# Feed-forward out-projections as seven block products, with weight block sums made by adding DMAs

## The chip, the cores and the metric

The kernel runs on one core of a Trainium2 chip, in one launch. The metric is the device time of one execution in microseconds. Before the change the median of three runs is 1543.88 us (1541.49 to 1548.66). The engines are TensorE (PE, with its weight loads shown as PEld), VectorE (DVE), ScalarE (ACT), GpSimd (POOL) and SyncE (SP). DMAs are put on a queue by SP, ACT or POOL, and sixteen DMA engines carry them.

## The reference, cut to what matters

The model is a two-layer streaming encoder over 640 frames: 512 of a prompt and 8 x 16 of running streams. Layer 0 is a convolution module, layer 1 is banded attention; each is followed by a SwiGLU feed-forward block. Everything is float32.

```python
D_MODEL, SEQ, DEPTH, DEC_BATCH, DEC_SEQ = 1024, 512, 2, 8, 16
FFN_HIDDEN = 2816                       # 22 tiles of 128

def swiglu_ffn(h, g, w_in, w_out):      # once in each layer
    a, b = jnp.split(rms_norm(h, g) @ w_in, 2, axis=-1)
    return h + (jax.nn.silu(a) * b) @ w_out
```

So each feed-forward block multiplies 640 x 1024 by 1024 x 5632 (the in-projection), gates, and multiplies 640 x 2816 by 2816 x 1024 (the out-projection).

## The kernel before, in words

The residual `h` stays in SBUF, features on the partitions: 8 tiles of 128 features by 640 frames. The frames are handled as two halves of 320 columns.

Float32 accuracy comes from splitting. ACT rounds a tensor to a `hi` part in the matmul's fast float32 type, DVE subtracts it from the original and so makes the `lo` part (`hilo`, L319, and `xsplit`, L153). Every product is then three matmuls: hi by hi, lo by hi, hi by lo.

`ffn` (L284) runs once per layer. An inner tile is 128 of the 2816 hidden features, with its `a` and its `b` column of the in-projection; its weights are four blocks of 128 x 512 floats, one megabyte in all. The first three inner tiles (NSTD) are done plainly (`std`, L391: 96 matmuls each). The other 19 go through `seven` (L401). It treats the in-projection of one tile as a 2 x 2 by 2 x 2 block product, rows being `a` and `b`, columns being the two halves of the frames, and forms it from seven block products instead of eight: 7 x 4 x 3 = 84 matmuls of 128 x 320. That needs sums of weight blocks, made in `w_seven` (L339): one load of the raw megabyte, then four additions or subtractions of 512 columns on DVE (L352), then the split into hi and lo of all seven operands. The sums of the activations, XT1 to XT4, are made once per layer. The last two products of a tile are issued by `after`, inside the next tile's `seven`.

The out-projection is plain. The 22 inner tiles are done in groups of 6, 6, 6 and 4 (`F1`, L40, loop at L493). After a group's gated tiles are in place, its out-weights are loaded in five pieces, split, and `mm3` (L162) accumulates over the group for each of 8 output tiles and 2 halves; DVE adds each result from PSUM to `h` (L530). The last group's columns are cut by `tail` instead of by half.

Each engine runs its own instructions in order. The order is made at build time by a list scheduler with a model of times; `tc.high_priority` moves splits, gates and evictions forward. Raw weights have two buffers (`wp`, bufs=2), and so have the split ones; the six PSUM buffers `mm` hold the accumulators. SP issues the weight loads in order and waits before each until the last reader of the buffer, on DVE, is done.

Of the kernel before, what the change touches and what calls it, by code (L numbers as in the profile page):

```python
# [8 lines left out]
F32 = mybir.dt.float32  # L9
# [6 lines left out]
P = 128  # L16
# [23 lines left out]
F1 = ((0, 6), (6, 6), (12, 6), (18, 4))  # L40
# [17 lines left out]
CW = 6  # L58
# [15 lines left out]
def tile_trunk(ctx, tc, xT, vecs, hist, w_pw1, w_pw2, w_in0, w_out0, w_in1, w_out1,  # L74
# [11 lines left out]
    tw = [320]  # L86
    mm = tps.enter_context(tc.tile_pool(name="mm0", bufs=4, space=PSUM))
# [81 lines left out]
    def square(s, n, eng="a", q=None):  # L169
        if q is None:  # L170
            q = tp.tile([P, tw[0]], F32, tag="sq", name=nm("sq"))
# [10 lines left out]
    def colmean(st, pieces, n, cut, tag, eng=nc.gpsimd, accp=None):  # L182
# [3 lines left out]
        for s in pieces[:cut]:  # L186
# [3 lines left out]
            if acc is None:  # L190
                acc = accp or tp.tile([P, tw[0]], F32, tag="acc", name=nm("acc"), bufs=1)
# [92 lines left out]
    def ffn(l, w_in, w_out, tail, hf):  # L284
# [15 lines left out]
        bcw = xo.tile([P, NT], F32, name=nm("bcw"), tag="bcw")  # L300
# [6 lines left out]
        xb = ExitStack()  # L307
        xt = xb.enter_context(tc.tile_pool(name="xt", bufs=1, reuse_waits="tile"))

        def hidt(jj, dt=F32R):  # L310
            return [hpf.tile([P, 2, NH], dt, tag=f"h{t}{jj}", name=nm("hid")) for t in "hl"]
# [4 lines left out]
        def wsmall(n=1024, t="v"):  # L316
            return [wx.tile([P, n], F32R, tag=t + x, name=nm(t + x)) for x in ("hi", "lo")]

        def hilo(hi, lo, a, src):  # L319
            b = a + src.shape[-1]  # L320
            nc.scalar.activation(out=hi[:, a:b], in_=src, func=AF.Copy)  # L321
            nc.vector.tensor_tensor(out=lo[:, a:b], in0=src, in1=hi[:, a:b].bitcast(F32),  # L322
                                    op=ALU.subtract)

        def w_std(src, small):
            raw = wp.tile([P, 2048], F32, tag="raw", name=nm("raw"))
            ws = []
            for i in range(2):
                if small or i == 0:
                    hi, lo = (wsmall if small else wbig)()  # L330
                o = 0 if small else 1024 * i
                nc.sync.dma_start(raw[:, 1024 * i:1024 * i + 1024], src[:, 1024 * i:1024 * i + 1024])
                with tc.high_priority(offset=HP):
                    hilo(hi, lo, o, raw[:, 1024 * i:1024 * i + 1024])
                ws.append((hi, lo, o))
            return {X11: ws[0][:2] + (ws[0][2],), X21: ws[0][:2] + (ws[0][2] + 512,),
                    "b": (ws[1], ws[1][:2] + (ws[1][2] + 512,))}

        def w_seven(src):  # L339
            raw = wp.tile([P, 2048], F32, tag="raw", name=nm("raw"))  # L340
            nc.sync.dma_start(raw, src)
            a11, a12, a21, a22 = (raw[:, 512 * i:512 * i + 512] for i in range(4))
            s1 = wx.tile([P, 512], F32, tag="s1", name=nm("s1"), bufs=1)
            vh, vl = wsmall()
            uh, ul = wsmall(512, "u")
            gh, gl = wbig()
            sub, add = ALU.subtract, ALU.add
            with tc.high_priority(offset=HP):
                hilo(vh, vl, 0, raw[:, 0:1024])
                for out, x, y, op in ((s1, a21, a22, add), (a21, a11, a21, sub),  # L350
                                      (a11, s1, a11, sub), (a12, a12, a11, sub)):
                    nc.vector.tensor_tensor(out=out, in0=x, in1=y, op=op)  # L352
# [3 lines left out]
            return {X11: (vh, vl, 0), X21: (vh, vl, 512), X22: (gh, gl, 512), XT2: (gh, gl, 0),  # L356
                    XT1: (gh, gl, 1536), XT3: (gh, gl, 1024), XT4: (uh, ul, 0)}

        def product(pt, w, x, first):
            wh, wl, o = w  # L360
            for k in range(4):
                a, b = wh[:, o + k * P:o + k * P + P], wl[:, o + k * P:o + k * P + P]
                for i, (wt, v) in enumerate(((a, XH), (b, XH), (a, XL))):
                    nc.tensor.matmul(pt, wt, v[x][:, k, :], start=(first and k == i == 0),  # L364
                                     stop=(k == 3 and i == 2), skip_group_check=True)
# [10 lines left out]
        def plus(tag, kept, pt):  # L376
            t = ftmp(tag)
            with tc.high_priority(offset=HP):
                nc.vector.tensor_tensor(out=t, in0=pt, in1=kept, op=ALU.add)
# [6 lines left out]
        def gate(t, a, b, hid):  # L386
            with tc.high_priority(offset=HP):
                nc.vector.tensor_tensor(out=t, in0=a, in1=b, op=ALU.mult)
                xsplit(t, *hid)

        def std(ws, half, hid):  # L391
            pa, pb = mmt()[:, :NH], mmt()[:, :NH]
            for x, ka, kb in (((X11, X11, 0), (X21, X21, 1)), ((XT4, X11, 0), (X22, X21, 1)))[half]:
                product(pa, ws[ka], x, kb == 0)
                product(pb, ws["b"][kb], x, kb == 0)
# [820 lines left out]
```

## Time and profile before

| | |
|---|---|
| median of 3 runs | 1543.88 us |
| span of the profiled execution | 1541.4 us |
| PE busy in the span | 1480.1 us, 96% |
| DVE, ACT, POOL busy | 994.1, 668.7, 229.8 us |
| moved by DMA | 163.14 MB, mean 106 GB/s |
| PE clock granted, mean | 0.986 |

The profile's lines give engine, operation, tiles out<-in, shape, count, busy time and mean duration in ns, then how long the engine sat idle just before them and what ended that. A matmul's own duration is longer than the distance from one to the next, since they are pipelined: counts in a stretch of time tell the rate. Feed-forward of layer 0 lies at about 270 to 690 us of the span, that of layer 1 at about 1095 to 1530 us.

### The profile page before, as it was taken

Reading aid. Unit: us, or ns where it says so; the run is one execution under the profiler, and the core shown is the slowest. Engines: PE = TensorE matmul, PEld = TensorE weight load, DVE = VectorE, ACT = ScalarE, POOL = GpSimd, SP = SyncE. Lnnn points to the kernel's source line nnn. Section 1 sums busy time; section 2 is a strip of 40 time slices with the busy share of each in tenths; the row PEclk is TensorE's granted clock in tenths of the full one; section 3 lists DMA queues with packets and bytes.
Section 4 is the critical chain, followed back from the end, with each engine's and each line's share of the span. In section 5 each row is a group of like instructions: output and inputs, shape, how many; then the busy total and the mean of one; then the engine's idle time right before and its main releaser. Section 6 shows DMA issues by size and latency. Waiting matters only on the chain.

```text
span 1541.4 us, 27271 instructions
## 1 busy us (share of the span) xinstructions
PE 1480.1 (96%) x11190; PEld 1409.6 (91%) x11190; DVE 994.1 (64%) x1963; ACT 668.7 (43%) x1293; POOL 229.8 (15%) x250
## 2 busy tenths in 40 slices
PE   5999899999999999999999999988999999999997
PEld 5998689999999999999987798857899999999996
DVE  5799346775575575566776668553776575575556
ACT  3666245443353353344664355442544253253233
POOL 5789222000000000013121111111000000000001
PEclk9999899999999999999999999999899999999998
DMA  7167413013123123134555454460113123123211
GB/s 234 64 188 179 100 56 110 28 59 106 58 83 106 55 86 107 55 110 142 172 158 195 155 195 153 159 194 28 55 49 114 58 76 105 67 76 102 70 55 69
DMA packets 56316, 163.14 MB, mean 106 GB/s; under 512 B 10112, under 2 KB 25216, under 8 KB 47744
## 3 DMA queue, kind: packets, MB, share of 16 engines
q1 hardware_dynamic: 55904, 161.10, 32.6%
q8 instruction: 88, 1.44, 0.4%
q14 instruction: 36, 0.29, 0.1%
q10 hardware_dynamic: 288, 0.31, 0.1%
HBM read 149.78 MB, written 11.61 MB: 105 GB/s over the span
## 4 chain that ended last, share of the span: by engine, by line
PE 84%; POOL 5%; DVE 5%; DMA 2%; ACT 2%; issue 2%; POOLq 0%; DVEq 0%; ACTq 0%
PE mm L364 36%; PE mm L165 13%; PE mm L166 12%; PE mm L167 12%; POOL ca L639 4%; PE mm L677 2%; DMA cache<-in_ck 1%; PE w L201 1%; PE w L1013 1%; PE am L998 1%; PE am L981 1%; PE am L1044 1%; DVE w L626 1%; ACT whi L145 1%; PE w L957 1%
## 5 line engine op out<-in xcount | busy, mean ns | idle before, releaser
L364 PE MATMUL mm<-XH,wlo 128*128 128x320 f32 x736 | 228.9, 311 | 0.5 <-DVE wlo L322 0.5
L364 PE MATMUL mm<-XH,whi 128*128 128x320 f32 x736 | 227.9, 312 | 0.0
L364 PE MATMUL mm<-XL,whi 128*128 128x320 f32 x736 | 225.9, 310 | 0.0
L165 PE MATMUL mm<-xh,whi 128*128 128x320 f32 (+2 forms) x640 | 201.2, 316 | 4.3 <-ACT xh L154 2.6
L166 PE MATMUL mm<-xh,wlo 128*128 128x320 f32 (+2 forms) x640 | 200.2, 314 | 0.6 <-DVE wlo L149 0.6
L167 PE MATMUL mm<-xl,whi 128*128 128x320 f32 (+2 forms) x640 | 197.5, 313 | 0.0
L166 PE MATMUL mm<-hid,wlo 128*128 128x320 f32 (+2 forms) x560 | 172.1, 309 | 0.0
L167 PE MATMUL mm<-hid,whi 128*128 128x320 f32 (+2 forms) x560 | 169.6, 308 | 0.0
L165 PE MATMUL mm<-hid,whi 128*128 128x320 f32 (+2 forms) x560 | 167.9, 309 | 0.0
L321 ACT ACTIVATE whi<-raw 128x1536 fp32r<-128x1536 f32 (+2 forms) x90 | 100.9, 1148 | 122.4 <-PE mm L167 91.1
L322 DVE TENSOR_TENSOR wlo<-raw,whi 128x1536 fp32r<-128x1536 f32 (+2 forms) x90 | 118.6, 1341 | 39.6 <-ACT whi L321 39.4
L364 PEld LDWEIGHTS mm<-XH,wlo 128*128 128x128 f32 x736 | 139.5, 190 | 1.2 <-DVE wlo L322 1.2
L364 PEld LDWEIGHTS mm<-XH,whi 128*128 128x128 f32 x736 | 139.4, 190 | 0.0
L364 PEld LDWEIGHTS mm<-XL,whi 128*128 128x128 f32 x736 | 138.3, 189 | 0.0
L165 PEld LDWEIGHTS mm<-xh,whi 128*128 128x128 f32 x640 | 121.5, 190 | 7.8 <-ACT xh L154 3.1
L166 PEld LDWEIGHTS mm<-xh,wlo 128*128 128x128 f32 x640 | 121.8, 190 | 1.2 <-DVE wlo L149 0.8
L167 PEld LDWEIGHTS mm<-xl,whi 128*128 128x128 f32 x640 | 121.0, 190 | 1.2 <-issue 1.0
L364 PE MATMUL mm<-XH,vhi 128*128 128x320 f32 x368 | 115.4, 314 | 4.0 <-ACT XH L448 4.0
L364 PE MATMUL mm<-XL,vhi 128*128 128x320 f32 x368 | 114.5, 312 | 1.4 <-DVE XL L449 1.3
L364 PE MATMUL mm<-XH,vlo 128*128 128x320 f32 x368 | 115.3, 313 | 0.0
L166 PEld LDWEIGHTS mm<-hid,wlo 128*128 128x128 f32 x560 | 105.2, 188 | 0.0
L167 PEld LDWEIGHTS mm<-hid,whi 128*128 128x128 f32 x560 | 104.7, 188 | 0.0
(216 smaller groups left out, 3363.7 us busy)
## 6 DMA issues: line engine op xcount, KB each, us to landing
raw<-in_w_in SPq DMA_DIRECT2D x38, 1024.0 KB
cache<-in_ck SPq DMA_DIRECT2D x32, 512.0 KB
cache<-in_cv SPq DMA_DIRECT2D x32, 512.0 KB
raw<-in_w_out SPq DMA_DIRECT2D x18, 768.0 KB
raw<-in_w_pw SPq DMA_DIRECT2D x12, 1024.0 KB
raw<-in_w_kq SPq DMA_DIRECT2D x8, 1024.0 KB
raw<-in_w_in SPq DMA_DIRECT2D x12, 512.0 KB
raw<-in_w_out SPq DMA_DIRECT2D x12, 384.0 KB
```

The costliest lines, as they stand in the source:

```text
L145: nc.scalar.activation(out=hi[:, a:b], in_=raw[:, a:b], func=AF.Copy)
L165: nc.tensor.matmul(ps, wh, xh, start=(i == 0), stop=False)
L166: nc.tensor.matmul(ps, wl, xh, start=False, stop=False)
L167: nc.tensor.matmul(ps, wh, xl, start=False, stop=(i == last))
L201: nc.tensor.matmul(st[:, 512 + t * w + k:513 + t * w + k], s[:, a:a + P], onec, start=True, stop=True)
L321: nc.scalar.activation(out=hi[:, a:b], in_=src, func=AF.Copy)
L322: nc.vector.tensor_tensor(out=lo[:, a:b], in0=src, in1=hi[:, a:b].bitcast(F32), op=ALU.subtract)
L364: nc.tensor.matmul(pt, wt, v[x][:, k, :], start=(first and k == i == 0), stop=(k == 3 and i == 2), skip_group_check=True)
L626: nc.vector.scalar_tensor_tensor(out=dst, in0=src, scalar=wj, in1=dst, op0=ALU.mult, op1=ALU.add)
L639: nc.gpsimd.tensor_tensor(out=acc, in0=acc, in1=pr, op=ALU.add)
L677: nc.tensor.matmul(pt[32 * q:32 * q + 32, 0:n], w4[0:r, 4 * tg + q, :], mv, start=(tg == 0), stop=(tg == 7))
L957: nc.tensor.matmul(ps, QQ[:, q], KK[:, 0:n], start=True, stop=False)
```

## The change

The 22 inner tiles of a layer are now 3 plain ones, 16 in four chunks of four (`NCH`), and 3 at the end that go through `seven` but whose out-projection is plain.

For a chunk, the out-projection is also done by block products. Rows are pairs of output tiles, the inner blocks are the chunk's first and last two inner tiles, columns are the halves of the frames. `quad` does four output tiles with one megabyte of out-weights: seven products, each for two output rows `j`, of 2 x 3 matmuls, 84 in all, in the order `QORD`. It uses six PSUM accumulators. After each of the 14 products DVE adds or subtracts the accumulator into `h`; the accumulators go on collecting, so one value reaches several outputs. The activations' block sums are made by `combined`, per pair of inner tiles: seven splits for a pair, where `seven` before needed four.

All weight block sums, for `seven` and `quad`, are now made by DMA. `w_seven` loads the raw megabyte and, into a second buffer `e`, its first three blocks again. Then four DMAs on GpSimd's queue add one 128 x 512 block to another in place. The third adds the result of the first, and the fourth that of the third. The four DVE operations are gone; some sums now carry the other sign, and subtractions elsewhere (`gate`, `minus`) turn it back. The host gives the middle out-weights in the new order as `w_os`. The temporaries and hidden tiles are laid out anew (`unit`, `sqt`, `bcw`). The weights of the last two products (XT4 and X22) lie in tile `a`, which has one buffer.

```diff
-F1 = ((0, 6), (6, 6), (12, 6), (18, 4))
+NCH = 4
+QORD = ((5, 0), (5, 1), (1, 0), (1, 1), (2, 0), (2, 1), (6, 0), (6, 1), (3, 0), (7, 0), (3, 1),
+        (7, 1), (4, 0), (4, 1))
...
         def w_seven(src):
-            raw = wp.tile([P, 2048], F32, tag="raw", name=nm("raw"))
+            raw = wraw()
+            e = wx.tile([P, 1536], F32, tag="e", name=nm("e"))
+            w, s, a = wbig(), wsmall("s", 512), wsmall("a", 1024, 1)
             nc.sync.dma_start(raw, src)
...
+            nc.sync.dma_start(e, src[:, 0:1536])
             with tc.high_priority(offset=HP):
-                hilo(vh, vl, 0, raw[:, 0:1024])
-                for out, x, y, op in ((s1, a21, a22, add), (a21, a11, a21, sub),
-                                      (a11, s1, a11, sub), (a12, a12, a11, sub)):
-                    nc.vector.tensor_tensor(out=out, in0=x, in1=y, op=op)
-                hilo(gh, gl, 0, raw[:, 0:1536])
-                hilo(gh, gl, 1536, s1)
-                hilo(uh, ul, 0, a22)
+                for out, x in ((raw[:, 1024:1536], src[:, 1536:2048]),
+                               (e[:, 1024:1536], src[:, 0:512]),
+                               (e[:, 0:512], raw[:, 1024:1536]),
+                               (e[:, 512:1024], e[:, 0:512])):
+                    nc.gpsimd.dma_start(out, x, accum_op=add)
+                cut(w, 0, raw[:, 0:1024])
+                cut(w, 1024, e[:, 0:512])
+                cut(w, 1536, raw[:, 1024:1536])
+                cut(s, 0, e[:, 1024:1536])
+                cut(a, 0, raw[:, 1536:2048])
+                cut(a, 512, e[:, 512:1024])
+            return {X11: (w, 0), X21: (w, 512), XT2: (w, 1024), XT1: (w, 1536), XT3: (s, 0),
+                    XT4: (a, 0), X22: (a, 512)}
...
+        def combined(HH, HL, kp, second, held):
+            def own(c, src):
+                put(HH[c][:, kp, :], HL[c][:, kp, :], src)
+
+            def sink(half, a, b):
+                t = ftmp(f"B{half}{int(second)}", 1)
+                with tc.high_priority(offset=HP):
+                    gate(t, a, b)
+                    if half == 0:
+                        own((X11, X21)[second], t)
+                    elif not second:
+                        d = ftmp("b2")
+                        nc.vector.tensor_tensor(out=d, in0=held[0], in1=t, op=sub)
+                        own(XT1, d)
+                    else:
+                        b11, b12, b21 = held
+                        nc.vector.tensor_tensor(out=b12, in0=t, in1=b12, op=sub)
+                        minus(b11, b12, b11)
+                        own(XT2, b11)
+                        minus(b21, b11, b21)
+                        own(X22, t)
+                        own(XT3, b12)
+                        own(XT4, b21)
+                held.append(t)
+            return sink
...
+        def quad(src, m0, HH, HL):
+            ws = w_seven(src)
+            pe, pa, pb = ([mmt()[:, :NH] for _ in range(2)] for _ in range(3))
+
+            def go(pt, c, first, half, row, op, j):
+                product(pt[j], ws[c], HH[c], HL[c], first, 2, 256 * j)
+                for half, row, op in ((half, row, op),):
+                    hv = h[:, m0 + 2 * j + row, half * NH:half * NH + NH]
+                    with tc.high_priority(offset=HP):
+                        nc.vector.tensor_tensor(out=hv, in0=hv, in1=pt[j], op=op)
...
-        for j0, ch in F1:
...
+        for c in range(NCH):
...
+            for jj in range(4):
+                if jj % 2 == 0:
+                    held = []
+                after = seven(w_in[NSTD + 4 * c + jj], combined(HH, HL, jj // 2, jj % 2, held), after)
             after(0)
             after(1)
...
+            for q in range(2):
+                quad(w_os[2 * c + q], 4 * q, HH, HL)
```

More of the change, by code (lines that the diff above doesn't have):

```diff
@@ L306, in ffn, with unit @@
         hpf = hs.enter_context(tc.tile_pool(name="hpf", bufs=1, reuse_waits="tile"))
[L307 to L311, printed above, removed]
+        sqt[:] = "t3", "t2", 2
+        tw[0] = NH
+        bcw = wx.tile([P, 1536], F32, tag="e", name=nm("bcw"))
+        sub, add, mult = ALU.subtract, ALU.add, ALU.mult
+        def unit(i, dt=F32R):
+            return hpf.tile([P, 2, NH], dt, tag=f"u{i}", name=nm("hid"))
@@ L333, in w_std @@
+            for i in range(0, 2048, 1024):
+                nc.sync.dma_start(raw[:, i:i + 1024], src[:, i:i + 1024])
                 with tc.high_priority(offset=HP):
[L334 to L337, printed above, removed]
+                    n = 512 if small and i else 1024
+                    for j in range(i, i + 1024, n):
+                        cut(*ws[j // 512], raw[:, j:j + n])
@@ L356, in w_seven @@
[L356 to L365, printed above, removed]
+            nc.sync.dma_start(e, src[:, 0:1536])
@@ L500, in ffn, with idle @@
+        def idle(i):
+            pass
+        for c in range(NCH):
+            HH, HL = [None] * 7, [None] * 7
+            for i, x in enumerate((X21, XT4, X22, X11, XT1, XT2, XT3)):
+                HH[x], HL[x] = unit(2 * i), unit(2 * i + 1)
+            after = idle
+            for jj in range(4):
+                if jj % 2 == 0:
+                    held = []
+                after = seven(w_in[NSTD + 4 * c + jj], combined(HH, HL, jj // 2, jj % 2, held), after)
             after(0)
             after(1)
-            last = j0 + ch == FT
@@ L532, in ffn @@
+            for q in range(2):
+                quad(w_os[2 * c + q], 4 * q, HH, HL)
+        hids = [(unit(2 * jj), unit(2 * jj + 1)) for jj in range(NSTD)]
+        after = idle
+        for jj in range(NSTD):
+            after = seven(w_in[NSTD + 4 * NCH + jj], plain(hids[jj]), after)
+        after(0)
+        after(1)
+        ws = w_plain(NSTD, 0) + w_plain(NSTD, 4)
+        o_plain(hids, [(g, m, w) for g in tail for m, w in ws])
         hs.close()
```

215 lines of the change are left out of this document (115 added, 100 removed).

## The prediction

> **What bounds the kernel now.** I read the page's shares and chain first, then the table of stretches, then the groups of instructions by form, then single moments of the queues.
>
> ```profile
> PE 1480.1 (96%) x11190; PEld 1409.6 (91%) x11190; DVE 994.1 (64%) x1963; ACT 668.7 (43%) x1293; POOL 229.8 (15%) x250
> PE 84%; POOL 5%; DVE 5%; DMA 2%; ACT 2%; issue 2%; POOLq 0%; DVEq 0%; ACTq 0%
> core 0: us, PE busy (x) PEld busy (x) DVE busy (x) ACT busy (x) POOL busy (x), PEclk, DMA share, GB/s
> 400.00:500.00 100.00, 100.00 (x684) 100.00 (x683) 64.56 (x101) 42.34 (x71) 0.00 (x0) 1.00 0.26 85
> 280.00:680.00 400.00, 400.00 (x2727) 399.76 (x2726) 253.50 (x404) 156.62 (x256) 0.00 (x0) 1.00 0.23 74
> 1100.00:1510.00 410.00, 410.00 (x2788) 410.00 (x2787) 258.03 (x408) 160.69 (x261) 0.00 (x0) 1.00 0.22 73
> ```
>
> The chain that ended last is PE. In both feed-forward stretches PE never rests, at the full clock, while DVE works 64%, ACT 40%, POOL not at all and the DMA engines a quarter of the time. There the time is the count of matmuls: 100 us / 684 = 146.2 ns each. A removed matmul saves that as long as its operands stay early.
>
> **Matmuls removed.** The out-projection's count before:
>
> ```profile
> L166 PE MATMUL mm<-hid,wlo 128*128 128x320 f32 x432 | 132.8, 308 | 0.0
> L166 PE MATMUL mm<-hid,vlo 128*128 128x320 f32 x144 | 44.5, 309 | 0.0
> L166 PE MATMUL mm<-hid,wlo 128*128 128x384 f32 x64 | 21.5, 336 | 0.0
> L166 PE MATMUL mm<-hid,wlo 128*128 128x256 f32 x64 | 17.8, 282 | 0.0
> ```
>
> That is 704 of one of three kinds, so 2112, or 1056 per layer (22 inner tiles x 8 x 2 x 3). After it is 8 quads x 84 plus 6 plain inner tiles x 48, so 960. Two layers lose 192; the PE stream of the built program is also 192 shorter. 192 x 146.2 ns = 28.1 us, the most this change can give.
>
> **Work put on DVE and ACT.**
>
> ```profile
> L322 DVE TENSOR_TENSOR wlo<-raw,whi 128x1536 fp32r<-128x1536 f32 x38 | 66.8, 1758 | 31.6 <-ACT whi L321 31.4
> L352 DVE TENSOR_TENSOR raw<-raw 128x512 f32<-128x512 f32 x76 | 52.1, 685 | 0.6
> L322 DVE TENSOR_TENSOR vlo<-raw,vhi 128x1024 fp32r<-128x1024 f32 x42 | 51.1, 1223 | 12.3 <-ACT vhi L321 10.6 <-PE am L998 1.5
> L530 DVE TENSOR_TENSOR h<-mm,h 128x320 f32<-128x320 f32 x96 | 46.0, 488 | 58.3 <-PE mm L167 58.0
> L439 DVE SCALAR_TENSOR_TENSOR hid<-h,vec,bcw 128x320 f32<-128x320 f32 x24 | 11.4, 546 | 0.0
> L322 DVE TENSOR_TENSOR wlo<-raw,whi 128x768 fp32r<-128x768 f32 x36 | 32.9, 954 | 4.9 <-ACT whi L321 4.9
> L321 ACT ACTIVATE vhi<-raw 128x1024 fp32r<-128x1024 f32 x42 | 44.5, 1060 | 55.6 <-PE mm L167 33.0 <-PE mm L364 10.8 <-issue 7.1
> L321 ACT ACTIVATE uhi<-raw 128x512 fp32r<-128x512 f32 x38 | 24.0, 632 | 104.0 <-DMA raw<-in_w_in 57.2 <-PE mm L364 46.8
> L154 ACT ACTIVATE hid<-a 128x320 fp32r<-128x320 f32 x88 | 41.0, 466 | 64.5 <-DVE a L388 64.4
> ```
>
> Weights of one unit (a `seven` or a `quad`, 84 matmuls, 12.28 us of PE) took DVE 1.22 + 1.76 + 2 x 0.69 + 4 x 0.69 = 7.1 us; now 1.22 + 5 x 0.69 = 4.65 us. For 38 sevens that is -93 us, for 16 quads +74. The out-weights' own splits fall from 48 of 768 columns and 8 of 1024 to 16 of 768: -40. Evictions into `h` rise from 128 to 288: 160 x 0.488 = +78. A chunk makes 14 splits of gated tiles where 8 were: 48 x 0.488 = +23; 64 sums of 0.49 to 0.55 add 33. In all about +80 us on 994, 70% of the span. That average is covered by PE. A quad is not average: 4.65 + 14 x 0.488 = 11.5 us of DVE in 12.28. ACT cuts in six pieces: 1.06 + 5 x 0.63 = 4.2 us a unit, 38 x 0.4 + 16 x 4.2, less some 52 for the old out-weights, near +30 with 48 more splits x 0.47 = 23 on top; covered.
>
> Where a chunk ends there is a seam. After the last seven's last matmul the chain to XT2's operand is: sum 0.49, silu 0.47, gate 0.55, two sums 0.49 + 0.55, hi 0.47, lo 0.49 = 3.5 us; XT3's lo follows one more sum and two more lo, about 1.5 us, behind six evictions and some weight cuts that are due on DVE then, 3 to 4 us. PE has products XT1, X11, X21 in the quad to do meanwhile: 36 x 0.146 = 5.3 us. So 0 to 4 us of wait per chunk; I take 2.4, 8 chunks, 19 us.
>
> **The adding DMAs.** This is the term that decides, and no DMA of POOL's queue stands in the trace. The nearest are loads on SP's queue with a reader that waited for them:
>
> ```profile
> 366.36 0.33 SPq L341 DMA_DIRECT2D raw<-in_w_in  x1
> 371.14 0.63 ACT L321 ACTIVATE uhi<-raw 128x512 fp32r<-128x512 f32 x1 [3.89 <-DMA raw<-in_w_in]
> 353.13 0.33 SPq L507 DMA_DIRECT2D raw<-in_w_out  x1
> 356.16 0.85 ACT L321 ACTIVATE vhi<-raw 128x768 fp32r<-128x768 f32 x1 [2.15 <-DMA raw<-in_w_out]
> SPq L341 <- DVE wlo L322: 133.4, 9, 48.2
> ```
>
> 1024 KB take 4.78 us from issue to reader, 384 KB 3.03 us: 1.75 us for 640 KB, so 256 KB would take 2.7 us. An add reads its destination too; as 512 KB it would take 3.4 us. Call one add L. Ends: 2.7 us (a plain copy) and 4.8 us (it costs as much as the 1024 KB row, through its issue on POOL, its second read or the sharing below). I take 3.5 us, nearest to the 512 KB reading.
>
> Queues matter more than a single add. In the built order POOL issues the four adds of a unit in a row; the third waits for the first to land, the fourth for the third, and the next unit's first stands behind them. SP's next load waits for DVE's last reader of the buffer two units back (the last row shows that kind of wait), and that reader is the cut of tile `a`. On ACT the cut of `a` stands behind the next unit's cuts: in half of the units behind the one that waits for the third add, in the others behind the raw megabyte or the first add. So the prefetch of two buffers does not run free; per two units it is a loop:
>
> - load 4.8, first add L, third add L, hi of XT2 and of `a` 3 x 0.63, lo 0.69: 7.4 + 2L;
> - next load 4.8, hi 1.06, in half of the cases an add L and a hi 0.63, hi of `a` 2 x 0.63, lo 1.22 + 0.69: 9.3 + L/2.
>
> Sum 16.7 + 2.5 L, against 2 x 12.28 = 24.56 us of PE. At L = 2.7 it is 23.5 and hidden; at 3.5 it is 25.5.
>
> Bytes raise it. A unit moved 1024 KB; it now loads 1792 KB and adds 4 x 256 KB, 2.8 MB in 12.28 us, 235 GB/s where 85 were. The packets of a megabyte fill 3.4 us of the engines:
>
> ```profile
> DMA  0000000000091918799997996963000000000000
> GB/s 0 0 0 0 0 0 0 0 0 0 0 287 41 205 41 246 287 369 410 451 451 328 451 532 287 451 287 123 0 0 0 0 0 0 0 0 0 0 0 0
> ```
>
> (402 to 410 us, slices of 0.2 us, issue at 403.30.) 1792 KB fill 6 us of each 12.28, so half of the adds meet a load; where they do each gets half the engines, and a transfer of 0.7 to 1.4 us doubles: 0.3 us more per add on average, 0.6 per load. Over the loop 2.5 x 0.3 + 2 x 0.6 = 2 us. At L = 3.5 it is then 27.5 us, 2.9 over PE's, and the wait stands on PE because weights, evictions and splits share ACT's and DVE's order: an ACT cut that waits for an add holds back the silu and the splits behind it. The seam lies inside this wait then.
>
> At a block's start the first adds have the three plain tiles to hide under, 288 matmuls x 0.146 = 42 us; at its end the last plain out-projection has three inner tiles where it had four, and its loads are ready as before. I cost both at nothing.
>
> **Sum.** 48 units in chunks are 24 pairs x 2.9 = +70 us; -28.1 matmuls; +3 for the six plain sevens, whose loads start late after the plain phases. +45 us on the span of 1541.4 gives 1586; the median of the runs lies 2.5 us above the profiled span, so 1589.
>
> A page speaks for the change here. The Trainium skill, DMA: Bandwidth & Descriptors, section Anatomy of one DMA — SWDGE (gpsimd) path, fits a DMA of GpSimd's queue as 2.0 us + bytes / 436 GB/s, an estimate of 2.6 us for 256 KB; by it the loop is hidden and the first rival below holds. Another speaks against: Collectives: The Full Stack, section The bandwidth ceiling, says an add in a DMA needs two source reads on the same ring; no run here shows it yet.
>
> **Rivals.**
>
> Faster: L is near 2.7 us and meetings with loads are rare. The loop, 23.5 us, hides; what remains is -28 and the seam's 0 to 19: 1516 to 1535, say 1526. For it: the DMA engines idle three quarters of the time today, and all three engines have room on average. It turns at 16.7 + 2.5 L + 2 = 24.56 + 1.2 us (the 28 us spread over 24 pairs), that is L = 2.8 us.
>
> Same: the loop is over by about what the matmuls give, L of 2.8 to 2.9: 1536 to 1552.
>
> Much slower: an add costs 4.8 us or more. The loop is 16.7 + 2 + 12 = 30.7, +6.1 x 24 = 147, less 28: 1663 and above. POOL's own chain adds nothing yet: two landings and an issue, 2 x 4.8 + 1, are under a unit's 12.28. For it: an add does more than any row here, and POOL has issued no DMA so far. Against it: 256 KB is little.
>
> POOL held up by DVE: if each add, before it starts, waited out one DVE instruction, 0.5 to 1.2 us by the rows above, L would be 4.0 to 4.7 and the time 16.7 + 2 + 2.5 L against 24.56, so +4.1 to +5.9 per pair, 1614 to 1657. Chance 0.08. The Trainium skill, SBUF — State Buffer, section SBUF: two separate sides, describes this trap for a DMA of GpSimd's queue beside DVE operations in a two-port mode, and excepts two-input operations, which the rows here mostly are.
>
> **How the numbers follow.** What a measurement of this kernel can tell from no change is about 0.5%, 1536 to 1552. Paced by the adds as summed (L 3 to 4.5): 0.48, with its own range 1555 to 1650. Held up by DVE: 0.08. Much slower: 0.12. Faster: 0.22. Same: 0.10. The range goes from the faster case (1520) to the upper bound (1663), 1520 to 1663; it leaves out the ends of both.
>
> **What would show it.** PE's count 192 lower, its busy share in the feed-forward stretches at 85 to 90% instead of 100, with waits of 0.5 to 3 us on ACT's and DVE's cuts of `whi` and `ahi`, mostly in the quads; ACT's cuts waiting for DMAs of POOL's queue; the DMA share there 0.5 to 0.8. From one adding DMA's issue to the issue of the one that waits for it: L. If that is under 2.8 us, or if PE stays at 100%, I am wrong on the side of the rival; if PE's waits stand only at the seams, the adds are hidden and DVE is the price.

## The result, and the profile after

The changed kernel takes 1699.11 us in the median (1698.13 to 1699.52), the kernel before 1546.27 us beside it on the same chip: a ratio of 1.098, with a 95% interval of 1.095 to 1.101. That is 153 us slower. The forecast was 1589 us in a range of 1520 to 1663: the direction was right, the size was not.

The page of the changed kernel, busy time and chain:

```profile
PE 1518.1 (89%) x10998; PEld 1419.0 (84%) x10998; DVE 1046.6 (62%) x2217; ACT 723.0 (43%) x1475; POOL 420.0 (25%) x466
PE 38%; DMA 34%; DVE 10%; issue 8%; POOL 5%; ACT 5%; POOLq 0%; SPq 0%; DVEq 0%; ACTq 0%
DMA raw<-in_w_in 16%; PE mm L377 9%; DMA raw<-in_w_os 7%; PE mm L167 6%; PE mm L168 6%; PE mm L169 6%; DMA e<-raw 6%; POOL ca L716 4%; DVE wlo L318 2%; DVE alo L318 2%; ACT whi L317 1%; PE mm L754 1%; PE w L203 1%; DMA cache<-in_ck 1%; PE w L1091 1%
```

The 192 matmuls are gone (11190 to 10998). The chain that ended last was 84% PE; now a third of it is DMAs: weight loads and first adds, which both bear the names `raw<-in_w_in` and `raw<-in_w_os`, and the third add `e<-raw`. The stretches inside the feed-forward blocks (time; busy us and count of PE, PEld, DVE, ACT, POOL; granted clock; DMA share; GB/s):

```profile
400.00:500.00 100.00, 83.16 (x514) 79.26 (x514) 58.68 (x111) 38.52 (x73) 22.23 (x25) 0.91 0.76 190
280.00:680.00 400.00, 354.90 (x2273) 343.69 (x2271) 241.37 (x455) 159.56 (x298) 81.88 (x93) 0.94 0.68 169
1100.00:1510.00 410.00, 357.27 (x2320) 339.64 (x2320) 237.94 (x472) 156.27 (x295) 71.99 (x82) 0.93 0.59 146
```

PE issued 684 matmuls in 100 us and now issues 514. It idles 17% of the time, and its granted clock fell from 1.00 to 0.91. No engine is full and the DMA engines are at 0.76: this is a kernel that waits. Four of the longest waits of the whole span, those that end with a DMA of the feed-forward weights (engine, tile, line, what ended the wait; us in total, times, longest):

```profile
POOL e L362 <- DMA e<-raw: 229.6, 53, 9.7
ACT whi L317 <- DMA raw<-in_w_in: 157.4, 50, 7.2
POOL raw L362 <- DMA raw<-in_w_in: 154.4, 23, 20.9
ACT whi L317 <- DMA e<-raw: 96.4, 48, 6.5
```

The first row is GpSimd with the fourth add at the head of its queue, waiting for the third to land: 53 times, 4.3 us on average, up to 9.7 us. The DMA issues of the adds, with the median time from issue to landing at the end (256 KB each):

```profile
e<-raw POOLq DMA_DIRECT2D x54, 256.0 KB, 3.8
e<-e POOLq DMA_DIRECT2D x54, 256.0 KB, 3.4
e<-in_w_in POOLq DMA_DIRECT2D x38, 256.0 KB, 4.7
raw<-in_w_in POOLq DMA_DIRECT2D x38, 256.0 KB, 4.3
```

And here is the chain of waits through two rounds of the loop of two units (start, us, what; pieces are left out where "..." stands):

```profile
483.31 5.78 DMA raw<-in_w_os
...
489.74 4.28 DMA raw<-in_w_os
...
494.41 0.89 POOL e L362
495.30 9.07 issue
...
505.00 5.64 DMA raw<-in_w_in
...
511.03 3.90 DMA e<-raw
...
517.42 0.69 DVE alo L318
518.13 4.77 DMA raw<-in_w_in
...
523.55 4.26 DMA raw<-in_w_in
...
530.22 4.83 DMA raw<-in_w_in
...
535.71 5.09 DMA raw<-in_w_in
...
541.20 3.58 DMA e<-raw
...
548.61 4.99 DMA raw<-in_w_in
```

The second round, from 518.13 us on, is the loop that the prediction described: a load, the first add, in one of the two units the third add, then the cuts, the last of them `alo`, and with it the next load. The first round goes another way. Its third add was issued at 494.41, and GpSimd's queue went on at 504.36, after 9.07 us of "issue"; only then did the next unit's first add go out (505.00), and that unit's third add (511.03) waited for it. So this round runs through GpSimd's in-order queue and the adds of both units, and closes through the cut of `a`. From load to load over two units it is 518.13 - 483.31 = 34.8 us and 548.61 - 518.13 = 30.5 us; PE has 24.56 us of work in that time. The third add of the second round took 3.58 us. What the timeline has around the third add of the first round (start, duration, instruction; in brackets the idle time before it):

```profile
493.31 0.33 SPq L355 DMA_DIRECT2D raw<-in_w_in  x1
494.31 0.33 SPq L356 DMA_DIRECT2D e<-in_w_in  x1
...
505.05 0.64 PE L377 MATMUL mm<-hid,ahi 128*128 128x320 f32 x1 [7.59 <-ACT hid L317]
```

The raw and `e` loads of the next unit went out within 1.1 us before the add: it met both. From 496 to 499 us the DMA engines were busy 93% of the time and moved 126 packets of the loads' queue, but 7 of GpSimd's. PE's wait of 7.59 us is put down to ACT's split of a gated tile. That split has nothing to do with the adds; it stood in ACT's queue behind a cut that waited for `e<-raw`. After the wait the matmuls run slower for a while, and so they do after a shorter wait later in the trace:

```profile
505.05:508.50 3.45, 3.45 (x13) 3.45 (x14) 2.30 (x6) 0.94 (x2) 2.03 (x3) 0.50 0.61 92
508.50:512.00 3.50, 2.37 (x14) 1.85 (x13) 3.37 (x10) 2.01 (x3) 0.88 (x1) 1.00 0.82 139
...
563.10:566.50 3.40, 3.40 (x15) 3.40 (x14) 2.70 (x6) 2.13 (x6) 0.70 (x1) 0.50 0.97 351
```

```profile
562.06 0.41 PE L377 MATMUL mm<-XH,shi 128*128 128x320 f32 x1 [2.36 <-ACT t L389]
```

Between 505.05 and 508.50 us PE is busy all the time, yet issues 13 matmuls where the full clock gives 23; the granted clock is 0.50. The Trainium skill, TensorE: Matmul & The Clock Gate, section Part 1: The HAM clock gate, says that after about 3.4 us without work the array's clock is halved, and is given back after about as long of steady work. For this wait of 7.59 us the trace agrees, and the clock is back at 1.00 from 508.50 us on. But a wait of 2.36 us (559.70 to 562.06) was enough as well: the clock was 0.50 from 563.10 to 566.50. So the 3.4 us of the Trainium skill is no lower bound for a wait here; the measurement decides.

### The profile page after: what moved, and what is told of

Its sections match the earlier page's. It is cut to its first block, busy times and chain, and to the rows that moved or that the text cites. A ratio compares the mean times of both kernels' runs of the same rounds, so it can differ in the third digit from the quotient of the medians.

```text
span 1696.4 us, 28164 instructions
## 1 busy us (share of the span) xinstructions
PE 1518.1 (89%) x10998; PEld 1419.0 (84%) x10998; DVE 1046.6 (62%) x2217; ACT 723.0 (43%) x1475; POOL 420.0 (25%) x466
## 3 DMA queue, kind: packets, MB, share of 16 engines
q0 software_dynamic: 31104, 56.64, 20.5%
## 4 chain that ended last, share of the span: by engine, by line
PE 38%; DMA 34%; DVE 10%; issue 8%; POOL 5%; ACT 5%; POOLq 0%; SPq 0%; DVEq 0%; ACTq 0%
DMA raw<-in_w_in 16%; PE mm L377 9%; DMA raw<-in_w_os 7%; PE mm L167 6%; PE mm L168 6%; PE mm L169 6%; DMA e<-raw 6%; POOL ca L716 4%; DVE wlo L318 2%; DVE alo L318 2%; ACT whi L317 1%; PE mm L754 1%; PE w L203 1%; DMA cache<-in_ck 1%; PE w L1091 1%
## 5 line engine op out<-in xcount | busy, mean ns | idle before, releaser
L318 DVE TENSOR_TENSOR wlo<-raw,whi 128x1024 fp32r<-128x1024 f32 (+2 forms) x132 | 127.1, 973 | 173.2 <-ACT whi L317 172.8
L317 ACT ACTIVATE whi<-raw 128x1024 fp32r<-128x1024 f32 (+2 forms) x132 | 111.1, 855 | 262.1 <-DMA raw<-in_w_in 157.4
L377 PE MATMUL mm<-hid,whi 128*128 128x320 f32 x512 | 143.2, 343 | 26.1 <-ACT hid L317 7.1
L377 PEld LDWEIGHTS mm<-hid,whi 128*128 128x128 f32 x512 | 99.3, 210 | 37.7 <-DVE hid L318 11.0
L491 DVE TENSOR_TENSOR h<-h,mm 128x320 f32<-128x320 f32 x224 | 102.9, 482 | 23.6 <-PE mm L377 23.0
L377 PE MATMUL mm<-hid,ahi 128*128 128x320 f32 x256 | 72.5, 336 | 47.7 <-ACT hid L317 43.5
L377 PE MATMUL mm<-XH,ahi 128*128 128x320 f32 x336 | 104.9, 312 | 3.9 <-ACT t L389 3.2
L377 PE MATMUL mm<-XL,ahi 128*128 128x320 f32 x336 | 104.4, 311 | 0.7 <-DVE XL L318 0.7
L362 POOL DMA_DIRECT2D e<-e x54 | 47.4, 878 | 229.7 <-DMA e<-raw 229.6
L377 PE MATMUL mm<-XH,alo 128*128 128x320 f32 x336 | 104.1, 310 | 0.0
```

Of the source, the lines that this page charges most:

```text
L317: nc.scalar.activation(out=hi, in_=src, func=AF.Copy)
L318: nc.vector.tensor_tensor(out=lo, in0=src, in1=hi.bitcast(F32), op=sub)
L362: nc.gpsimd.dma_start(out, x, accum_op=add)
L377: nc.tensor.matmul(pt, wt, v[:, k, :], start=(first and k == i == 0), stop=(k == n - 1 and i == 2), skip_group_check=True)
L491: nc.vector.tensor_tensor(out=hv, in0=hv, in1=pt[j], op=op)
```

## The experiments

Two theories stood at the start, and a rival. *Loop*: the time goes to the chain add, add, cut, load that the prediction set up. *Products*: it goes to the block products themselves, their evictions, splits and the seams at chunk ends. *Traffic*: the second load and the double reads fill the DMA engines.

**Block products with the sums on VectorE (e1).**

```diff
-            nc.sync.dma_start(e, src[:, 0:1536])
-                    nc.gpsimd.dma_start(out, x, accum_op=add)          # four adds
+                for out, x, y in ((s1, a21, a22), (a21, a11, a21), (a11, s1, a11), (a12, a12, a11)):
+                    nc.vector.tensor_tensor(out=out, in0=x, in1=y, op=add)
```

> The block products for the out-projections stay; the four block sums of a weight go back to VectorE (four additions of 128x512 each), the second load and the adding DMAs go, and the small buffer of the first two blocks has two copies again. Loop theory (the time went to the chain add, add, add, cut, load): without adds the loop is gone, what is left is 28 us less TensorE, 10 to 20 us of seams at the chunk ends and up to 27 us where VectorE has 13.95 us of work in a quad unit of 12.28: 1532 to 1560 us. Products theory (the time went to evictions, splits and seams of the block products): it stays at 1660 us or above. Traffic theory (the second load and the adds' double reads fill the DMA engines): 1532 to 1560 as well, since both go.

Measured: 1566.4 us, ratio 1.015 (1.012 to 1.018). Products falls as the main cause: 133 of the 153 us are gone with the adds and the second load. But the change without them still doesn't pay. In a stretch of this run:

```profile
400.00:500.00 100.00, 96.52 (x643) 95.66 (x643) 87.86 (x152) 44.47 (x69) 0.00 (x0) 0.98 0.23 74
```

VectorE is at 88% on average there, so in the quads, by the 13.95 us in 12.28 of the expectation, over 100%. That this is what costs the 20 us left over is argued from the count; no run tests it.

**The changed kernel without the adds (e2).**

```diff
-                    nc.gpsimd.dma_start(out, x, accum_op=add)          # four adds left out
```

> The changed kernel without the four adding DMAs: the second load stays, and the blocks are cut as they were loaded, so the block sums are left out of what is computed. Loop theory: no chain, 1520 to 1545 us. Products theory: 1660 us or above. Traffic theory: the loads alone move 1.75 MB per 12.28 us unit, about 145 GB/s; if they are late by themselves, 1580 us or more, with waits of the cuts on the loads.

Measured: 1542.5 us, ratio 0.999 (0.997 to 1.001). So the adds cost 157 us, all of the loss and a little more; the second load costs little at most. This is also the most that this form of the change, with its buffers, cuts and second load, can give: with sums that cost nothing it is level with the kernel before. One chunk (four `seven` and two `quad`, 504 matmuls; the counts have two or three more at the edges), first in the changed kernel, then in this run:

```profile
487.24:581.77 94.53, 80.14 (x506) 77.12 (x505) 56.02 (x106) 37.19 (x70) 21.29 (x24) 0.93 0.74 184
```

```profile
465.81:541.70 75.89, 74.69 (x507) 73.88 (x505) 55.52 (x107) 36.69 (x71) 0.00 (x0) 1.00 0.40 146
```

A chunk is 18.6 us longer with the adds; eight chunks make 149 of the 157 us. Of the 18.6 us, 13.2 are idle time of PE (94.53 - 80.14 against 75.89 - 74.69), and 5.4 are longer busy time for the same matmuls (80.14 against 74.69). Of these, some 3.4 us are the half clock: the two rows above with a clock of 0.50, 6.85 us of work, lie in this chunk. This split is no sum of causes. The chain that ended last has no piece of PE in this chunk, so the slower matmuls are not shown to have made it longer.

**The first two blocks in the small buffer (e3).**

```diff
-                cut(w, 0, raw[:, 0:1024])
+                cut(a, 0, raw[:, 0:1024])
...
-                cut(a, 0, raw[:, 1536:2048])
-                cut(a, 512, e[:, 512:1024])
+                cut(w, 0, raw[:, 1536:2048])
+                cut(w, 512, e[:, 512:1024])
```

> The changed kernel with two cut destinations exchanged: the first two blocks of a weight go into the single small buffer (a), which the unit's first third reads, and the two blocks that are read last go into the double one (w). The cut that frees a raw buffer then no longer waits for the last product of the unit before. Loads, adds and products are the same. Loop theory (the wait of that cut closes the loop): a raw buffer is free after load 5 + four adds of about 4.7 + cuts 2 = 26 us at the earliest, which two units of 24.56 nearly cover: 1560 to 1620 us. Traffic theory: same bytes, same adds, 1670 us or above. Products theory: 1680 to 1700 us.

Measured: 1672.9 us, ratio 1.085 (1.079 to 1.090), a gain of 26 us where the loop theory wanted 80 or more. The loop through the cut of `a` is gone, and something else holds the units. The chain of this run names it, GpSimd's own queue:

```profile
488.53 5.79 DMA raw<-in_w_in
...
494.71 0.87 POOL e L362
495.59 8.30 issue
...
505.22 6.03 DMA raw<-in_w_in
```

One unit's adds take the queue from 488.53 to 505.22: 16.7 us, where PE needs 12.28. The first lands after 5.8 us, the third after 8.8, because it meets the next loads; only then does the fourth go out, and the next unit's first add, whose data are there, stands behind it. The median landing of the third add was 3.8 us in the changed kernel and is 7.1 here:

```profile
e<-raw POOLq DMA_DIRECT2D x54, 256.0 KB, 7.1
```

**The adds alone, in the kernel before (e4).**

```diff
-                for out, x, y, op in ((s1, a21, a22, add), (a21, a11, a21, sub), ...):
-                    nc.vector.tensor_tensor(out=out, in0=x, in1=y, op=op)
+                    nc.gpsimd.dma_start(out, x, accum_op=add)          # the four adds, with the load of e
```

> The kernel before with its plain out-projections, but each block product unit's sums formed by the second load and the four adding DMAs, with the small buffer in one copy and the cuts as in the changed kernel; all four sums are additions, so they carry other signs than the reference needs. Loop theory: the 38 block units run in pairs of about 33 us in place of 24.56, less what the out-projection stages between give the buffers to catch up: 1640 to 1700 us. Traffic theory: about the same, 1640 to 1700 us. Products theory: the sums cost nothing, 1530 to 1560 us.

Measured: 1610.8 us, ratio 1.043 (1.039 to 1.046): the adds hurt without any block product of the out-projection, +65 us on 38 units. That is less than expected. The likely reason, which no run tests, is that the plain out-projection after each group gives the buffers time to fill.

**Smaller loads (e5).**

```diff
-            nc.sync.dma_start(raw, src)
+            for j in range(0, 2048, 512):
+                nc.sync.dma_start(raw[:, j:j + 512], src[:, j:j + 512])     # and e in three pieces
```

> The changed kernel with its two loads cut into pieces of 512 columns: seven loads of 256 KB in packets of 2 KB in place of one of 1 MB and one of 0.75 MB in packets of 8 and 6 KB. Adds, cuts and their order are the same. Turns theory (an add that meets loads lasts 7 to 10 us in place of 3.3 because its 8 packets on each DMA engine take turns with load packets of 8 KB, 309 ns each): with 84 ns packets the third add falls to 4 us or less on average, and the time to 1600 to 1660 us. Bytes theory (the adds wait because the engines are full, whatever the packets): 1690 to 1710 us, third add still near 4.9.

Measured: 1738.2 us, ratio 1.123 (1.120 to 1.127), worse than either theory said. The third add's median is 4.0 us, not lower, and ACT's wait for the raw load or the first add, which bear one name, grew from 157 to 196 us:

```profile
ACT whi L317 <- DMA raw<-in_w_in: 196.3, 56, 6.7
e<-raw POOLq DMA_DIRECT2D x54, 256.0 KB, 4.0
```

That the packets' size makes the meeting long is not borne out; why seven loads are worse than two stays open.

**Plain copies in place of the adds (e6).**

```diff
-                    nc.gpsimd.dma_start(out, x, accum_op=add)
+                    nc.gpsimd.dma_start(out, x)
```

> The changed kernel with plain copies in place of the four adds (same sources, sizes, queue and waits; the block sums are left out of what is computed). What is taken away is the second read alone. Queue theory (four transfers that wait for each other in one in-order queue, each with a fixed part of 2 to 3 us beside its packets): each landing gets 0.7 to 1 us shorter, 1620 to 1670 us. Double-read theory (the accumulation itself is the cost): 1545 to 1580 us.

Measured: 1618.8 us, ratio 1.047 (1.044 to 1.050). This is just under the range of the queue theory and well above that of the other. Same queue, waits and orders on all engines; half of the loss goes with the accumulation, the second read above all (GpSimd's issue of one is shorter too, 0.55 us in place of 0.88). The landings:

```profile
e<-e POOLq DMA_DIRECT2D x54, 256.0 KB, 2.4
raw<-in_w_in POOLq DMA_DIRECT2D x38, 256.0 KB, 3.3
```

Each is 1 us shorter. In GpSimd's queue as a whole (packets, MB, share of 16 engines' span), the changed kernel and then this one:

```profile
q0 software_dynamic: 31104, 56.64, 20.5%
```

```profile
q0 software_dynamic: 17280, 56.64, 10.9%
```

For the same 56.64 MB the adds take 0.205 x 16 x 1696.4 / 56.64 = 98 us of engine time per MB, the copies 0.109 x 16 x 1621.3 / 56.64 = 50. The sentence of the Trainium skill on two source reads (Collectives: The Full Stack, section The bandwidth ceiling), which the prediction held against the change, is written there of the add in a reduce-scatter; the doubled engine time here agrees with it. The Trainium skill's fit of 2.6 us for 256 KB (DMA: Bandwidth & Descriptors, section Anatomy of one DMA — SWDGE (gpsimd) path) is near the copies out of SBUF (2.4 us); copies out of HBM took 3.3 us, adds 3.4 and 4.3 us, and by these the kernel runs.

**The third and fourth sum on VectorE (e7), and this together with e3 (e9).**

```diff
-                    nc.gpsimd.dma_start(out, x, accum_op=add)          # e[0:512], e[512:1024]
+                    nc.vector.tensor_tensor(out=out, in0=out, in1=x, op=add)
```

> The changed kernel with the third and fourth sum, which need the first's result, on VectorE; GpSimd's queue keeps the two adds that read only what was loaded. Queue theory: no add waits for another add, the queue's work per unit falls from some 15 us to under 8, and the time to 1550 to 1590 us. If the loads and the first adds (4.2 to 6 us each) hold the loop, 1640 us or more.

Measured: 1671.3 us, ratio 1.081 (1.078 to 1.084): 28 us gained, where the queue theory wanted over 100. Taking away the `a` loop gave 26, taking away the dependent adds 28. The 28 are not clean: VectorE's sums wait in its queue for the first add here, 62.3 us in all for those out of `in_w_in`. From this came the two-loops theory, that either loop alone holds a unit at 15 us or more.

> Both half-measures at once: the first two blocks in the single small buffer (which alone gave 1673), and the third and fourth sum on VectorE (which alone gave 1671). Two-loops theory (the changed kernel stands in two loops of 15 to 16 us a unit each, the wait of the cut of a behind the next unit's add, and the four adds in GpSimd's in-order queue, so that taking away either leaves the other): with both gone a unit needs load 5 + add 5 + two sums 1.4 + cuts 3 = some 15 us of the 24.56 that two buffers give, and the time is 1550 to 1585. One-cause theories (total bytes, double reads, second load): the two gains of 27 us add up at best, 1640 us or more.

Measured: 1669.9 us, ratio 1.079 (1.077 to 1.082). A plain miss; nothing was gained by doing both. But in this version the wait in VectorE's queue is longer still:

```profile
DVE e L362 <- DMA raw<-in_w_in: 112.3, 30, 5.3
```

and its chain runs through it (an add, the sum that waited for it, an eviction behind the sum, then PE):

```profile
505.62 4.24 DMA raw<-in_w_in
...
509.89 0.69 DVE e L362
510.58 0.41 DVE h L491
...
511.03 12.52 PE mm L377 x73
```

The sum stood at the head of VectorE's queue until the add had landed, and evictions that PE needed stood behind it. So this run could not decide on the two loops.

**Copies together with e3 (e10).** The edits of e3 and e6.

> The first two blocks in the single small buffer, and plain copies in place of the four adds (the sums are left out of what is computed), still in the same order in GpSimd's queue. Two-loops theory: the queue needs 0.65 + 3.3 + 1.3 + 3.5 + 1.5 = some 10 us a unit with copies, under 12.28, and the other loop is gone: 1545 to 1575 us. If it's the bytes of loads and transfers that bound the units: the same bytes in one read less, near the 1619 of the copies alone.

Measured: 1552.5 us, ratio 1.004 (1.002 to 1.006). Now nearly the whole loss is gone, with the same bytes loaded, four transfers per unit in the same queue, and the same orders as e3 on every engine. Its chunk:

```profile
467.05:544.18 77.13, 75.26 (x507) 73.93 (x505) 56.11 (x106) 36.48 (x70) 12.90 (x25) 1.00 0.67 226
```

The DMA engines carry 226 GB/s here, more than the 184 of the changed kernel. So bytes as such are no bound. In engine time the traffic theory is not ruled out as neatly. A unit of the changed kernel takes 0.74 x 94.53 / 6 = 11.7 us of all the DMA engines, of e2 0.40 x 75.89 / 6 = 5.1, of this version 0.67 x 77.13 / 6 = 8.6. With four adds the engines would be 95% full at PE's pace of 12.28 us. They are at 74% as the kernel runs, so this is not what holds it alone; but no run has the adds' full engine time without the two loops, and it may well be the next limit behind them.

**The same square without VectorE (e12, e13).** The third and fourth sum as instructions of GpSimd, with the cuts of e3 (e12) and of the changed kernel (e13).

```diff
-                    nc.gpsimd.dma_start(out, x, accum_op=add)          # e[0:512], e[512:1024]
+                    nc.gpsimd.tensor_tensor(out=out, in0=out, in1=x, op=add)
```

> The first two blocks in the single small buffer, and the third and fourth sum as instructions of GpSimd (1.5 us each) in place of adding DMAs: the same queue, but its chain is 1.3 + 5 + 3 us a unit in place of 15 to 16, and VectorE's queue gets no wait for an add (which the version with these two sums on VectorE had). Two-loops theory: both loops are gone and nothing takes their place, 1550 to 1590 us. If the loads and the first two adds alone are too slow for two buffers (load 5 + e load 1.5 + add 5 + sums 3 + cuts 3 = 17.5 of 24.56 us by rows, so they should not be): 1640 us or more, as with the sums on VectorE.

> The same two sums as instructions of GpSimd, but the cuts as in the changed kernel, so the cut that frees a raw buffer still waits behind the next unit's add. Two-loops theory: this loop is left, 1640 to 1690 us, as with the two sums on VectorE. If the chain in GpSimd's queue was the whole cause: 1550 to 1590 us here as well.

Measured: e12 1592.5 us, ratio 1.029 (1.025 to 1.032), just outside what was expected; e13 1657.9 us, ratio 1.072 (1.069 to 1.075), as expected. Medians in us:

| | four adds as DMAs | last two on GpSimd itself | plain copies |
|---|---|---|---|
| cut of `a` last, as changed | 1699 | 1658 | 1619 |
| first blocks in `a` (e3) | 1673 | 1593 | 1552 |

Going down gains 26 us while the queue holds the four adds, and 65 or 66 once its chain is shorter. Going right gains 41 and 80 us in the upper row, 80 and 120 in the lower. Each step is worth more when the other has been taken, as with two loops of about the same length, one behind the other. They are not quite separate: with both in place the kernel is slower than with either alone (1699 against 1673 and 1658), and the first round of the chain above runs through both. The steps down leave bytes and transfers as they are. The steps to the right also lighten the DMA engines, so how much of them is the shorter queue and how much the lighter traffic stays open. What e12 still has over e2, 50 us, is partly another matter, which the next run shows.

**The sums as instructions of GpSimd (e8).** The version e1 with its four additions moved.

```diff
-                    nc.vector.tensor_tensor(out=out, in0=x, in1=y, op=add)
+                    nc.gpsimd.tensor_tensor(out=out, in0=x, in1=y, op=add)
```

> The version with VectorE's sums, but with the four additions of 128x512 on GpSimd as instructions (1.52 us each by the row of the same shape before, 6.1 us per 12.28 us unit, no second load, no adding DMA). If GpSimd is only another adder: VectorE is as free as without sums, 1530 to 1550 us. If its three dependent additions (4.6 us) come late for the cuts, or the two engines hinder each other: 1565 us or more.

Measured: 1581.1 us, ratio 1.022 (1.020 to 1.025), slower than with the sums on VectorE. One form of VectorE's instructions, in e1 and then here:

```profile
L318 DVE TENSOR_TENSOR hid<-B,hid 128x320 fp32r<-128x320 f32 x96 | 46.3, 482 | 0.0
```

```profile
L486 DVE TENSOR_TENSOR h<-h,mm 128x320 f32<-128x320 f32 x224 | 100.0, 479 | 22.8 <-PE mm L372 22.5
L318 DVE TENSOR_TENSOR hid<-B,hid 128x320 fp32r<-128x320 f32 x96 | 81.3, 847 | 1.1
```

```profile
L318 DVE TENSOR_TENSOR hid<-B,hid x96: 474/489/1589, 354.9 to 1480.4; 128x320 fp32r<-128x320 f32 x96
```

The last row has the shortest, the median and the longest time of the same instructions, in ns. A subtraction of two tiles in SBUF takes 847 ns on average in place of 482, but the median is 489: the 32 of the 96 that run beside a GpSimd addition take 1576 ns, the other 64 take 483. An addition with one input in PSUM stays at 479. The Trainium skill, SBUF — State Buffer, section Who interferes with whom, says that a VectorE instruction with two SBUF inputs contends with a GpSimd instruction that reads SBUF; the rows agree. So VectorE is as busy as before, 87% from 400 to 500 us where e1 had 88%. Whether this or the late results of the dependent additions makes the 15 us over e1, the run does not separate.

**A mixed version (e11).** Sums of `seven` on VectorE; in `quad` the first two by adding DMAs, the others on VectorE; first blocks in `a`.

> A version to keep: sums of the in-projections on VectorE (which has 5 us to spare in their units), and in the quad units, where VectorE has none, the first two by adding DMAs and the other two on VectorE; first two blocks in the single small buffer, second load for the quads alone. If the two loops were the whole cost of the adds: 1540 to 1562 us, VectorE's overrun in the quads gone. If adds are late also where only two of six units have them: 1575 us or more.

Measured: 1597.0 us, ratio 1.033 (1.031 to 1.035), worse than e1. Here too VectorE's sums wait for adds, with other work of VectorE behind them, 55.4 us in all in the 16 quads. No version beat the kernel before, and by e2 there is little to win in this form: with free sums it is level.

**Half the columns (e14).** As e3, each add over 256 of its 512 columns.

> The first two blocks in the single small buffer, all four adds as DMAs, but each over 256 of its 512 columns (the sums of the other columns are left out of what is computed): as many bytes read per add as by the plain copy of 512 columns. If an add costs what its two reads cost: landings near the copies' 3.1 (first) and 2.3 us (fourth), and the time near the 1552 of the copies. If accumulation has a fixed price of its own: landings of 3.6 us or more undisturbed, and 1590 us or more.

Measured: 1569.6 us, ratio 1.015 (1.010 to 1.019), between the two. Median landings:

```profile
e<-e POOLq DMA_DIRECT2D x54, 128.0 KB, 2.8
raw<-in_w_in POOLq DMA_DIRECT2D x38, 128.0 KB, 3.5
```

An add of 128 KB lands like a copy of 256 KB or a little later (2.8 against 2.4, 3.5 against 3.4 in e10). So most of an add's price is its two reads, with up to 0.4 us beside that.

## Why the prediction was wrong, point by point

**The bound and the matmuls removed: right.** PE bound the stretches; 192 matmuls fell away.

**Work on VectorE and ACT, and the seam: right in size.** VectorE's busy time rose by 53 us where some 80 were worked out, ACT's by 54 where 53 were. The seam was put at 2.4 us a chunk; e2's chunk is 75.89 us where 6 x 12.28 = 73.7 would do, so 2.2. With -28 for the matmuls, e2 should then be some 10 us under the kernel before. It is 3 under, and where the other 7 went stays open.

**The faster rival: wrong.** It needed an add of 2.8 us or less. No kind of add has a median under 3.4.

**The adding DMAs: here it failed.** The loop of two units was put at 27.5 us. A chunk of three such pairs took 94.53 us, 31.5 a pair: 24 x (31.5 - 24.56) = 167 us in place of 70, and these 97 us are most of the 110 by which the forecast of 1589 was short. The loop that the prediction set up is there, 30.5 us long: load, first add, third add in half of the units, cuts, next load. Two of its terms were too small, and a path was missing.

- L, from one add's issue to the issue of the one that waits for it, was taken as 3.5 us. In the round of 30.5 us, where no add met the next unit's loads for long, the first add of the second unit took 5.09 and the third 3.58 us to land; with 0.65 us between a load's landing and the first add's issue, and 0.39 before the third's, that is 5.7 and 4.0, or 4.9 in the mean. The term 2.5 L is 12.2 us in place of 8.75, and the loop without meetings 28.9. The first add reads one operand from HBM and runs beside the end of its own unit's `e` load, which the estimate from a plain load's bytes did not show, and the gaps at GpSimd were not counted.
- Meetings were put at 0.3 us an add. In one of the two rounds the third add alone was held up by 6 us (9.07 + 0.89 from issue to the next piece, against 3.58 + 0.39). The sum took the meeting as an even sharing of the engines for the transfer's own 0.7 to 1.4 us; in the trace the add lands only when most of the loads have gone through.
- GpSimd's queue was left out as a path. In the round of 34.8 us the next unit's first add stands behind the fourth add, which waits for the third, and so the adds of both units follow each other in the chain.

**The much slower rival came nearest, and its side remark was wrong.** At L = 4.8 us it gave 1663. Its loop of 30.7 us is near the 31.5 measured, by an L near the 4.9 of the trace. It said that GpSimd's own chain adds nothing, "two landings and an issue" being under a unit's 12.28. e3 shows this chain at 16.7 us, since the meeting falls into it. That is why curing the loop through `a` gave 26 us only. In the changed kernel both hold at once, and I had looked for one.

**VectorE holding up GpSimd's DMAs: no row shows it clearly.** Of GpSimd's 768 us of waits before an add, 577 end with another DMA. The other 191 us, 48 waits, are put down to a VectorE instruction, 67 us of it in two waits at the start of a block; whether VectorE held these up or had merely finished last stays open. The issues themselves show no such thing: those of the third and fourth add take 857 to 902 ns, all 108 of them.

**The packets of a load.** The 3.4 us that the prediction read for a megabyte are the time over which its packets stand. e2's two loads, 1792 KB, take 5.1 us of the engines a unit where 6 were said.

**What would show it.** The share of PE in the stretches is 83 to 89% (85 to 90 said) and the DMA share 0.59 to 0.76 (0.5 to 0.8 said), but the waits reach 7.6 us where up to 3 were said.

## What to carry to other kernels

Price a transfer that others wait for by its time from issue to landing while the loads it will run beside are under way, and add the gap on the issuing queue: here an add of 256 KB in place took 3.4 to 5.2 us in the median, by kind, and up to 10 us beside loads, four a unit, against 0.69 us each on VectorE. When such transfers depend on each other in an in-order queue with two buffers, look for every loop through them, also those that pass from one queue to another, and test by removing loops in pairs: one alone can gain little while another of the same length stands behind it. Before building on a cheaper way to make operands, run the version that leaves them out; here it would have shown that hardly anything could be won.

## What the runs showed of the hardware

- A DMA with an add takes twice the engine time per byte of a copy (98 against 50 us per MB), and a copy on GpSimd's queue out of HBM lands some 0.9 us later than one out of SBUF (3.3 against 2.4 us).
- A small transfer that is issued beside loads of 1 MB and 0.75 MB on another queue can land only with them, 9 to 10 us after issue; smaller pieces of the loads did not help.
- A VectorE subtraction of two 128x320 tiles in SBUF that runs beside a GpSimd addition takes 1576 ns in place of 483 (e8), so the average hangs on how many meet one; those with a PSUM input stay at 479.
- After waits of PE of 7.59 and 2.36 us some 3.4 us of its work ran at a granted clock of 0.50: 13 matmuls in 3.45 us where 23 fit. In the chunk where this was seen PE is not in the chain, so that it cost time there is not shown.
